# A seven-product gate/up block with a row's sign turned: weight sums as pure additions, two of four made by accumulating DMAs

## The chip, the cores and the metric

The kernel runs on one core of a Trainium2 chip. The metric is device time in microseconds (us) of one execution, the median of several. Five engines work side by side, each with its own queue that runs in order: TensorE (PE, matmuls), VectorE (DVE), ScalarE (ACT), GpSimd (POOL) and SyncE (SP, which here only issues DMAs). Semaphores order work between engines.

## The reference

The reference is one layer of a hybrid trunk: a Mamba-2 part and a latent-attention part side by side, an output projection, and a dense SwiGLU feed-forward part, run for 512 prompt tokens and 64 sample tokens. All data is float32. What matters here is the feed-forward part, with D_MODEL = 1024 and D_FF = 2816:

```python
hf = rmsnorm(x, p['norm_ffn'])
x = x + (jax.nn.silu(hf @ p['w_gate']) * (hf @ p['w_up'])) @ p['w_down']
```

## The kernel before

**Layout.** The 576 tokens lie along the free axis and the model dimension along the 128 partitions. D_FF is cut into 22 tiles of 128, f = 0 to 21. The token axis is cut into two halves of 288.

**Float32 from two parts.** Each matmul operand is split into a high part (a cast to float32r by ACT, line 112) and a low part (what is left, by DVE, line 113). A product is then three matmuls: high by high, high by low, low by high. `split_weights` makes the two parts of a [128, 1024] weight block; their tiles are called `wh_...` and `wl_...`.

**The block form.** For a tile f, gate and up of both token halves are a 2x2 by 2x2 block product: rows are gate and up, the inner blocks are the even and the odd blocks of the model dimension, and the columns are the token halves. The kernel does it with seven block products in place of eight. Call the weight blocks A11, A12 (gate, even and odd) and A21, A22 (up). Four weight sums are needed:

- S1 = A21 + A22 (line 809, left half of tile `s1`)
- S3 = A21 − A11 (line 810, left half of tile `s2`)
- S2 = S1 − A11 (line 811, right half of `s1`)
- S4 = A12 − S2 (line 812, right half of `s2`)

All four are DVE instructions of 128x512. `gu_weights(f)` loads the up row (tile `r2`, line 806) and then the gate row (`r1`, line 807), 512 KB each, both from SP, makes the sums, and splits three groups of two blocks: (A11, A12), called `gu_A`, then (S1, S2) and then (S3, S4), both shown as `gu_S`; A22 is split by itself into `gu_a` (lines 814 and 820). The sums of the activations are made once, in `x_operands` (lines 783 to 801).

**Order of the products.** `gu_steps(f)` gives the steps of a tile: m1 (A11), then m4 (A22) and m3 (S4) of the tile before, which are done late, then m6 (S2), m7 (S3), m2 (A12) and m5 (S1). m1, m6, m5 and m3 add up in one PSUM bank, `ps_x`, with a copy (ACT: L914, L918) or an add (DVE: L931, L939) between them; m7 and m4 share `ps_z`; m2 has `ps_y`. Each product is 12 matmuls of 288 columns, so a tile has 84.

**Parts.** CUTS = (0, 5, 10, 14, 18, 22) groups the tiles in parts. After each part follows its down projection (lines 953 and 966), whose weights `wr_d` SP loads too; its results are added to x2 by DVE (L966). After the last part come the last norm and the outputs.

**Buffers.** Raw rows and sums share a pool of seven [128, 1024] slots, `wpool`; the split parts share eleven slots, `w2pool`. A load waits until the slot that it reuses is free, that is, until the split that read it last is done. For f = 0 the raw tiles come from `w2pool`.

**What sets the order.** Each engine runs its instructions in one fixed order. `ISSUE` lists the first stretch of it by hand for each engine (PE up to about the first three tiles of gate/up, and the like for DVE, ACT, POOL and SP); behind that, the tile scheduler orders the rest at build time from its own estimate of durations. POOL has little to do here: DMAs and memsets early, and part of the last norm. A DMA issued from POOL goes through POOL's software queue.

Of the kernel before, what the change touches and what calls it, by code (L numbers as in the profile page):

```python
# [14 lines left out]
ALU = mybir.AluOpType  # L15
# [4 lines left out]
P = 128  # L20
# [34 lines left out]
def hybrid_layer_kernel(ctx: ExitStack, tc: tile.TileContext, a, o):  # L55
    nc = tc.nc
    pe, act, dve, pool, sp = nc.tensor, nc.scalar, nc.vector, nc.gpsimd, nc.sync
# [6 lines left out]
    def close(p):  # L64
        p.__exit__(None, None, None)
# [3 lines left out]
    wpool = ctx.enter_context(tc.tile_pool(name="wpool", bufs=7))  # L69
# [10 lines left out]
    def tmp(name, w=T):  # L80
        return tpool.tile([P, UPW], F32, tag="t", name=name)[:, :w]

    def halves(ap):
        return ap.rearrange("p (a b) -> p a b", a=2)
# [14 lines left out]
    def col(c):  # L99
        return par[:, c : c + 1]  # L100
# [4 lines left out]
    def wslot(wp, name, dt=F32):  # L105
        return wp.tile([P, 1024], dt, tag="w", name=name)

    def split_weights(raw, name, wp=None):

        n = raw.shape[1]  # L110
        hi, lo = (wslot(wp or wout[0], f"{z}_{name}", F32R)[:, :n] for z in ("wh", "wl"))
        act.copy(hi, raw)  # L112
        dve.tensor_tensor(lo, raw, hi.bitcast(F32), ALU.subtract)  # L113
        return hi, lo
# [122 lines left out]
    for z, n, v, k0 in ((0, T, -1e30, 0), (1, NKEY, 1.0, 64)):  # L237
        m = qk_bufs[0][z][96:100]
        pool.memset(m, v)
        for sign in (1, -1):  # L240
            pool.affine_select(
                out=m, in_=m, pattern=[[0, 2], [sign, n]], compare_op=ALU.is_ge, fill=0.0,
# [53 lines left out]
    for hf in range(2):  # L296
        cols = slice(hf * TH, (hf + 1) * TH)
        for z, r0, n in ((k1, 0, 24), (k2, 32, 16)):
            r = slice(64 * hf + r0, 64 * hf + r0 + n)
# [26 lines left out]
    dt, e, s1, qq, acc = g1("dt"), g1("sp_e"), g1("sp_s"), g1("sp_q"), g1("sp_a")  # L326
# [427 lines left out]
    def load_x2():  # L754
# [8 lines left out]
        ORDER_ATT, g=gate, N=norm_y, y=cat_tile, X=load_x2, S=scores, T=turn, t=turn_s, V=values, W=values_s,  # L763
# [11 lines left out]
    w2pool = ctx.enter_context(tc.tile_pool(name="w2pool", bufs=11, reuse_waits="tile"))  # L775
# [7 lines left out]
    def x_operands(kp):  # L783
        last = len(xops) == 3
        if last:
            close(y_)
            pl = ctx.enter_context(tc.tile_pool(name="xop_last", bufs=1, reuse_waits="tile"))
        z = (pl if last else xop).tile([P, 2, 7, TH], F32, name=f"xop{kp}")
        zr = z.bitcast(F32R)
        e, d, t13, t24 = (tmp(f"xv{kp}_{i}").rearrange("p (a b) -> p a b", a=2) for i in range(4))  # L790
        for i, v in enumerate((e, d)):
            act.activation(v, halves(x2[2 * kp + i]), AF.Identity, scale=col(C_NF + 2 * kp + i))
        dve.tensor_tensor(t13[:, 0], e[:, 1], e[:, 0], ALU.subtract)
        dve.tensor_tensor(t13[:, 1], e[:, 1], d[:, 1], ALU.subtract)
        dve.tensor_tensor(t24[:, 0], d[:, 1], t13[:, 0], ALU.subtract)
        dve.tensor_tensor(t24[:, 1], d[:, 0], t24[:, 0], ALU.subtract)
        for v, r in ((e[:, :1], XB11), (d, XB21), (t13, XT1), (t24, XT2)):
            r = slice(r, r + v.shape[1])
            act.copy(zr[:, 0, r], v)
            dve.tensor_tensor(zr[:, 1, r], v, z[:, 0, r], ALU.subtract)  # L800
        xops[kp] = zr

    def gu_weights(f):

        r1, r2, s1, s2 = (wslot((w2pool, wpool)[f > 0], f"gu{f}_{z}") for z in range(4))
        sp.dma_start(r2, a["w_gu"][f, :, 1])
        gu_dma.append(sp.dma_start(r1, a["w_gu"][f, :, 0]).ins)
        l, r = (lambda z: z[:, :512]), (lambda z: z[:, 512:])
        dve.tensor_tensor(l(s1), l(r2), r(r2), ALU.add)
        dve.tensor_tensor(l(s2), l(r2), l(r1), ALU.subtract)  # L810
        dve.tensor_tensor(r(s1), l(s1), l(r1), ALU.subtract)
        dve.tensor_tensor(r(s2), r(r1), r(s1), ALU.subtract)
        a22 = wslot(w2pool, f"gu{f}_a22", F32R)
        act.copy(l(a22), r(r2))
        out = {"A22": (l(a22), r(a22))}
        for names, w in (("A11", "A12"), r1), (("S1", "S2"), s1), (("S3", "S4"), s2):
            w = split_weights(w, f"gu{f}_{names[0]}", wp=w2pool)
            for i, n in enumerate(names):
                out[n] = tuple(z[:, 512 * i : 512 * i + 512] for z in w)
        dve.tensor_tensor(r(a22), r(r2), l(a22).bitcast(F32), ALU.subtract)  # L820
        return out

    w_gu, squared, gu_dma = {}, [], []
# [22 lines left out]
    def block_product(ps, w, i, kps=KPS, first=True, last=True, onto=False):  # L846

        n, xi = PRODUCTS[i - 1]
        for kp in kps:
            (whi, wlo), x = wk(w[n], kp), xops[kp][:, :, xi]  # L850
            for j, (p, q) in enumerate(((whi, x[:, 0]), (whi, x[:, 1]), (wlo, x[:, 0]))):
                pe.matmul(  # L852
                    ps, p, q, start=not onto and first and kp == kps[0] and j == 0,
                    stop=onto or (last and kp == kps[-1] and j == 2), skip_group_check=onto,
                )

    def fbank(tag, name):
        return bank(tag, name)[:, :TH]
# [5 lines left out]
    def combine(i, ps, g, u):  # L864

        gl, gr, ul, ur = g[:, :TH], g[:, TH:], u[:, :TH], u[:, TH:]
        if i == 1:
            act.copy(gl, ps)
            return
        for out, other in {6: ((ul, gl),), 2: ((gl, gl),), 5: ((ur, ul),), 3: ((gr, ur),), 7: ((ur, ur), (ul, ul)), 4: ((ul, ul),)}[i]:  # L870
            dve.tensor_tensor(out, other, ps, ALU.add)

    ORDER = (1, 6, 2, 5, 3, 7, 4)

# [22 lines left out]
    def finish(f, g, u):  # L897
        act.activation(g, g, AF.Silu)
        dve.tensor_tensor(u, u, g, ALU.mult)
        s = slot(cpool, "c", f"pr{f}")  # L900
        split_scaled(s, u, None)
        prod[f] = hilo(s)

    def gu_steps(f):


        w = w_gu.pop(f) if f in w_gu else gu_weights(f)
        g, u = tmp(f"g{f}"), tmp(f"u{f}")
        gl, gr, ul, ur = g[:, :TH], g[:, TH:], u[:, :TH], u[:, TH:]
        x, y, z = fbank("sc", f"ps_x{f}"), fbank("pp", f"ps_y{f}"), fbank("pp", f"ps_z{f}")  # L910

        def m1():
            block_product(x, w, 1)
            act.copy(gl, x)  # L914

        def m6():
            block_product(x, w, 6, onto=True)
            act.copy(ul, x)  # L918

        def m7():  # L920
            block_product(z, w, 7)
            act.copy(ur, z)

        def m2():
            block_product(y, w, 2)
            dve.tensor_tensor(gl, y, gl, ALU.add)
            dve.tensor_tensor(gl, gl, R2[:, :TH], ALU.mult)

        def m5():
            block_product(x, w, 5, onto=True)  # L930
            dve.tensor_tensor(ur, x, ur, ALU.add)  # L931

        def m4():
            block_product(z, w, 4, onto=True)
            dve.tensor_tensor(ul, z, ul, ALU.add)

        def m3():
            block_product(x, w, 3, onto=True)
            dve.tensor_tensor(gr, x, R2[:, TH:], ALU.mult)  # L939
            finish(f, g, u)  # L940

        return m1, (m4, m3), (m6, m7, m2, m5)

    wout[0] = w2pool
# [87 lines left out]
    ps = [lbank(tag, f"ps_l0_{t}", 0) for t, tag in enumerate(("hm", "hm", "sc", "pp"))]  # L1032
    for t in range(4):
        down_half(ps[t], last_terms(t)[:-1], parts[0], True, False)
    for t in range(KT):
        if t < 4:
            p = ps[t]
            down_half(p, last_terms(t)[-1:], parts[0], False, True)
        else:
            p = lbank(("hm", "sc", "pp")[t % 3], f"ps_l0_{t}", 0)  # L1040
            down_half(p, last_terms(t), parts[0])
        add(t, 0, p)
        z = sql[:, parts[0]] if t == 1 else tmp("sq", parts[0].stop)
# [25 lines left out]
    with tc.manual_schedule(engines={pe.engine, dve.engine, pool.engine, act.engine}):  # L1069
        pn0, pn1 = lbank("sc", "ps_n3_0", 0), bank("pp", "ps_n3_1")[:, : len(BL)]  # L1070
        first, second, _ = norm_steps(pn0, pn0, D, eps=False)
# [10 lines left out]
        for t in range(KT):  # L1082
            p = lbank(("hm", "sc", "pp")[t % 3], f"ps_l1_{t}", 1)
# [20 lines left out]
        first, second, _ = norm_steps(Rt, pn1, D, eps=False)  # L1104
# [32 lines left out]
def issue_in_order(tc, nc):  # L1137
# [45 lines left out]
292-293 296 309 312 304 326 305 310 308 313 327 362 311 328 322 301 323 314 363 330 324 320 329 315 336 321 325 364  # L1183
333 367 337 331-332 365 340 338 334-335 341 344 349 339 345 350 342 346 352 351 343 355 358 366 347 359 357 348 360
356 353 361 368 377 354 370-371 369 372 375-376 373-374 382 390 378 384 383 385-386 379 389 387 380 397 388 381 393
405 395 391 396 398 394 392 400 399 401 403 402 420 406 404 408 407 409 412 410 417 414 411 413 418 462 416 421 423
419 464 425 422 424 415 433 431 426 432 429 428 427 438 430 434 469 463 436 435 437 439 442 441 443 466 440 444 451
465 446 467-468 452-453 445 447 455 454 448 473 475 456 477 476 474 457 472 470 478 458 449 479 488 459 490 485 492
480 489 491 471 450 503 481 505 493-494 482 460 495 487 500 507 504 496 506 518 461 508 502 510 568 575 545 509 512
483 525 511 497 520 519 501 522 486 484 573 521 515 513 517 548 523-524 570 498 530 537-538 527 543 516 526 565 499  # L1190
542 528 555 540 560 514 529 532 553 547 552 557 533 562 541 539 534 550 577 558 531 563 579 578 544 580 535
""",
    "ACT": """
0-5 8 6-7 10 9 13 11 14 12 15 17-18 16 21 19 24 20 23 40 22 25 44 26-27 51 28-33 48-49 55 34-35 37 36 59 50 41-42
# [10 lines left out]
350 359 375 370 367 369 368 376-378 371 379-380  # L1205
""",
    "POOL": """
0-3 7 18 28 4 8 5 9 6 10 26 11 27 12 29 13-17 20-23 19 24-25 31 30 32-42 53 55 57 59 54 56 58 60 43-52 61-73
""",
    "SP": """  # L1210
11-14 16 15 17-20 23 22 25 21 24 31 26 32 39-40 36 33 38 41-42 37 43-47 55 77 62 79 54 56 58 63 81 57 60 59 61 68 66
# [102 lines left out]
```

## Time and profile before

| | |
|---|---|
| median of 3 runs | 654.88 us (653.42 to 655.2) |
| span of the profiled execution, first to last instruction | 651.7 us |
| mean granted TensorE clock | 0.997 |
| PE, DVE, ACT, POOL busy | 639.9, 512.4, 339.3, 41.3 us |
| DMA traffic | 63.22 MB, mean 97 GB/s |

The page gives the profiled execution's time as its span, 651.7 us; some 3.2 us of the median lie outside the first and last instruction. A row of an engine's timeline has the start in us, the duration in us, the engine, the line, the operation, the tiles as out<-in, the shape and the count; in brackets stands how long the engine had been idle before it and which instruction ended that. A row of a group of instructions has count and mean duration; a row of DMA issues has the size of one and the median time from issue to landing.

### The profile page before, as it was taken

The numbers are of one execution on the slowest core, as the hardware profiler recorded it, in microseconds if no ns is written. First come the engines' busy times: TensorE is split into PE (matmuls) and PEld (weight loads), VectorE is DVE, ScalarE is ACT, GpSimd is POOL, SyncE is SP. The second block draws the span as 40 slices with busy tenths as digits, with TensorE's granted clock in tenths as the row PEclk, the third lists the DMA queues.
The fourth block names the chain that finished last, engine by engine and source line by source line (L and its number), as shares of the span: only waits on it lengthen the run. The fifth ranks groups of instructions, "written<-read, shape, count | busy, mean of one in ns | idle before, by whom it ended". The sixth has DMA issues, their size and how long they took to land.

```text
span 651.7 us, 11921 instructions
## 1 busy us (share of the span) xinstructions
PE 639.9 (98%) x4731; PEld 611.8 (94%) x4731; DVE 512.4 (79%) x935; ACT 339.3 (52%) x630; POOL 41.3 (6%) x80
## 2 busy tenths in 40 slices
PE   9999999998999999999999999999999999999995
PEld 8898989885787899999999999999999999999995
DVE  6899987899776699999996776775768577876655
ACT  7645426769674567665523445223533345334364
POOL 1321104001010000000000000000000000000023
PEclk9999999999999999999999999999999999999998
DMA  8312375323220232133422233311232224222004
GB/s 314 127 62 70 93 171 143 113 66 129 86 76 33 99 102 92 65 109 103 131 80 97 79 101 101 110 66 65 81 114 98 98 66 128 68 98 98 2 1 145
DMA packets 26151, 63.22 MB, mean 97 GB/s; under 512 B 3418, under 2 KB 10088, under 8 KB 25840
## 3 DMA queue, kind: packets, MB, share of 16 engines
q1 hardware_dynamic: 24560, 60.77, 28.3%
q0 software_dynamic: 816, 1.13, 0.8%
q8 instruction: 37, 0.61, 0.4%
q10 hardware_dynamic: 720, 0.57, 0.3%
q14 instruction: 18, 0.15, 0.1%
HBM read 58.03 MB, written 3.30 MB: 94 GB/s over the span
## 4 chain that ended last, share of the span: by engine, by line
PE 84%; DVE 3%; ACT 1%; DMA 1%; issue 1%; POOL 0%; POOLq 0%; DVEq 0%; ACTq 0%
PE ps_x L852 21%; PE ps_d L953 18%; PE ps_z L852 10%; PE ps_o L443 8%; PE ps_y L852 5%; PE ps_in L128 4%; PE ps_z L443 3%; PE ps_l L953 3%; PE ps_p L852 2%; PE sc L657 2%; PE pv L704 1%; PE ptp L679 1%; PE ps_v L590 1%; PE ps_q L443 1%; PE ps_y L527 1%
## 5 line engine op out<-in xcount | busy, mean ns | idle before, releaser
L953 PE MATMUL ps_d<-pr,wh_d 128*128 128x288 f32 x576 | 115.4, 294 | 0.0
L852 PE MATMUL ps_x<-xop,wh_gu_S 128*128 128x288 f32 x504 | 101.8, 295 | 0.0
L953 PEld LDWEIGHTS ps_d<-pr,wh_d 128*128 128x128 f32 x576 | 92.5, 188 | 0.0
L953 PE MATMUL ps_d<-pr,wl_d 128*128 128x288 f32 x288 | 84.6, 295 | 0.0
L852 PEld LDWEIGHTS ps_x<-xop,wh_gu_S 128*128 128x128 f32 x504 | 80.6, 188 | 0.2
L113 DVE TENSOR_TENSOR wl_gu_S<-gu,wh_gu_S 128x1024 fp32r<-128x1024 f32 x44 | 53.6, 1224 | 34.4 <-PE ps_y L852 13.8
L852 PE MATMUL ps_x<-xop,wl_gu_S 128*128 128x288 f32 x252 | 73.4, 295 | 0.0
L112 ACT CAST wh_gu_S<-gu 128x1024 fp32r<-128x1024 f32 x44 | 46.3, 1052 | 48.4 <-PE ps_d L953 25.4
L953 PEld LDWEIGHTS ps_d<-pr,wl_d 128*128 128x128 f32 x288 | 54.0, 188 | 0.0
L852 PEld LDWEIGHTS ps_x<-xop,wl_gu_S 128*128 128x128 f32 x252 | 47.0, 188 | 0.0
L128 PE MATMUL ps_in<-xs,wh_in 128*128 128x288 f32 x256 | 45.2, 298 | 1.2 <-DVE sp_a L351 1.0
L112 ACT CAST wh_d<-wr_d 128x640 fp32r<-128x640 f32 (+1 forms) x32 | 21.5, 673 | 39.1 <-PE ps_x L852 14.8
L128 PEld LDWEIGHTS ps_in<-xs,wh_in 128*128 128x128 f32 x256 | 37.5, 188 | 2.3 <-ACT up L381 1.2
L852 PE MATMUL ps_z<-xop,gu_a 128*128 128x288 f32 x252 | 38.0, 296 | 0.0
L852 PE MATMUL ps_z<-xop,wh_gu_S 128*128 128x288 f32 x168 | 36.0, 296 | 0.0
L852 PE MATMUL ps_x<-xop,wh_gu_A 128*128 128x288 f32 x168 | 35.3, 298 | 0.0
L852 PEld LDWEIGHTS ps_z<-xop,gu_a 128*128 128x128 f32 x252 | 35.1, 188 | 0.0
L852 PE MATMUL ps_y<-xop,wh_gu_A 128*128 128x288 f32 x168 | 34.2, 294 | 0.0
L966 DVE TENSOR_TENSOR x<-ps_d,x 128x288 f32<-128x288 f32 x64 | 28.8, 453 | 6.7 <-PE ps_d L953 6.5
L112 ACT CAST wh_gu_A<-gu 128x1024 fp32r<-128x1024 f32 x22 | 23.1, 1049 | 17.5 <-PE ps_d L953 11.5
L113 DVE TENSOR_TENSOR wl_gu_A<-gu,wh_gu_A 128x1024 fp32r<-128x1024 f32 x22 | 26.9, 1223 | 5.2 <-PE ps_x L852 3.9
L1049 POOL TENSOR_TENSOR fz<-fz,sq 128x320 f32<-128x320 f32 x3 | 2.6, 880 | 445.3 <-ACT sq L1044 445.3
(339 smaller groups left out, 1643.7 us busy)
## 6 DMA issues: line engine op xcount, KB each, us to landing
gu<-in_w_gu SPq DMA_DIRECT2D x44, 512.0 KB, 3.7
wr_d<-in_w_down SPq DMA_DIRECT2D x16, 320.0 KB, 2.9
wr_in<-in_w_in SPq DMA_DIRECT2D x8, 512.0 KB, 4.0
wr_out<-in_w_out SPq DMA_DIRECT2D x8, 512.0 KB, 3.2
wr_d<-in_w_down SPq DMA_DIRECT2D x16, 256.0 KB, 2.7
cumb<-cumD SPq DMA_DIRECT2D x5, 512.0 KB, 4.6
x<-in_xT SPq DMA_DIRECT2D x2, 1152.0 KB, 7.5
wr_z<-in_w_in SPq DMA_DIRECT2D x4, 512.0 KB, 4.4
```

Source lines behind the costliest of these rows:

```text
L112: act.copy(hi, raw)
L113: dve.tensor_tensor(lo, raw, hi.bitcast(F32), ALU.subtract)
L128: pe.matmul(ps[:m, hf, :n], w, x[:, hf * n : (hf + 1) * n], start=start and k == 0 and i == 0, stop=stop and k == last and i == 2,)
L443: pe.matmul(ps[:, :n], w, x[:, cols], start=k == 0 and i == 0, stop=k == len(terms) - 1 and i == 2,)
L527: pe.matmul(py[64 * j : 64 * j + 64, p * P : p * P + L], xdt[:L, h * HD : (h + 1) * HD], wts[:L, h, :L], start=True, stop=True,)
L590: pe.matmul(ps[:n], l, r, start=j == 0, stop=j == 2)
L657: pe.matmul(s[:, :nk], qs[:, j, q0 : q0 + P], ks[:, j, :nk], start=True, stop=True)
L679: pe.transpose(pp[:, k : k + P], prs[p, i][:, j, b * P : b * P + P], ident)
L704: pe.matmul(pv[64 * j : 64 * j + 64, b * P :], V[b][:, h * HD : (h + 1) * HD], pts[p, b, j], start=b == 0, stop=True, skip_group_check=b > 0,)
L852: pe.matmul(ps, p, q, start=not onto and first and kp == kps[0] and j == 0, stop=onto or (last and kp == kps[-1] and j == 2), skip_group_c ...
L953: pe.matmul(ps, w, x[:, cols], start=first and k == 0 and i == 0, stop=last and k == len(terms) - 1 and i == 2,)
L966: dve.tensor_tensor(x2[t][:, cols], ps, x2[t][:, cols], ALU.add)
```

## The change

A row's sign in the block form is turned, so that all four weight sums become additions: S3 = A21 + A11, S1 = A21 + A22, S2 = S1 + A11, S4 = A12 + S2. The activations' sums and the places where products are folded take the opposite signs (in `x_operands`, `combine`, m5 and m4).

For f = 1 and up, two of the sums are made by DMA. SP loads the left half of the up row (A21) twice, side by side, into a tile `s31`. Then two DMAs on POOL's queue read the left half of gate (A11) and the right half of up (A22) from DRAM and add them onto the left and the right half of `s31`, which then holds S3 and S1. SP loads the gate row (`r1`) as before, and of the up row only the right half (`r2`). DVE makes S2 and S4 in tile `s24`. The groups are split in the order (A11, A12), (S3, S1), (S2, S4). For f = 0 DVE makes all four sums, with the groups as before.

The lists in `ISSUE` are renumbered for the 42 instructions fewer on DVE; POOL's list has its last part renumbered, and the 42 accumulating DMAs are not in it.

```diff
@@ x_operands
-        dve.tensor_tensor(t13[:, 0], e[:, 1], e[:, 0], ALU.subtract)
+        dve.tensor_tensor(t13[:, 0], e[:, 0], e[:, 1], ALU.subtract)
         dve.tensor_tensor(t13[:, 1], e[:, 1], d[:, 1], ALU.subtract)
-        dve.tensor_tensor(t24[:, 0], d[:, 1], t13[:, 0], ALU.subtract)
-        dve.tensor_tensor(t24[:, 1], d[:, 0], t24[:, 0], ALU.subtract)
+        dve.scalar_tensor_tensor(t24[:, 0], t13[:, 0], -1.0, d[:, 1], ALU.mult, ALU.subtract)
+        dve.tensor_tensor(t24[:, 1], d[:, 0], t24[:, 0], ALU.add)
@@ gu_weights
-        r1, r2, s1, s2 = (wslot((w2pool, wpool)[f > 0], f"gu{f}_{z}") for z in range(4))
-        sp.dma_start(r2, a["w_gu"][f, :, 1])
-        gu_dma.append(sp.dma_start(r1, a["w_gu"][f, :, 0]).ins)
         l, r = (lambda z: z[:, :512]), (lambda z: z[:, 512:])
-        dve.tensor_tensor(l(s1), l(r2), r(r2), ALU.add)
-        dve.tensor_tensor(l(s2), l(r2), l(r1), ALU.subtract)
-        dve.tensor_tensor(r(s1), l(s1), l(r1), ALU.subtract)
-        dve.tensor_tensor(r(s2), r(r1), r(s1), ALU.subtract)
+        if f:
+            r1, r2, s31, s24 = (wslot(wpool, f"gu{f}_{z}") for z in range(4))
+            g, u = a["w_gu"][f, :, 0], a["w_gu"][f, :, 1]
+            sp.dma_start(s31.rearrange("p (a b) -> p a b", a=2), l(u).unsqueeze(1).to_broadcast([P, 2, 512]))
+            gu_dma.append(sp.dma_start(r1, g).ins)
+            pool.dma_start(l(s31), l(g), accum_op=ALU.add)
+            pool.dma_start(r(s31), r(u), accum_op=ALU.add)
+            sp.dma_start(r(r2), r(u))
+            dve.tensor_tensor(l(s24), r(s31), l(r1), ALU.add)
+            dve.tensor_tensor(r(s24), r(r1), l(s24), ALU.add)
+            sums = (("S3", "S1"), s31), (("S2", "S4"), s24)
+        else:
+            r1, r2, s1, s2 = (wslot(w2pool, f"gu{f}_{z}") for z in range(4))
+            sp.dma_start(r2, a["w_gu"][f, :, 1])
+            gu_dma.append(sp.dma_start(r1, a["w_gu"][f, :, 0]).ins)
+            dve.tensor_tensor(l(s1), l(r2), r(r2), ALU.add)
+            dve.tensor_tensor(l(s2), l(r2), l(r1), ALU.add)
+            dve.tensor_tensor(r(s1), l(s1), l(r1), ALU.add)
+            dve.tensor_tensor(r(s2), r(r1), r(s1), ALU.add)
+            sums = (("S1", "S2"), s1), (("S3", "S4"), s2)
         a22 = wslot(w2pool, f"gu{f}_a22", F32R)
         act.copy(l(a22), r(r2))
         out = {"A22": (l(a22), r(a22))}
-        for names, w in (("A11", "A12"), r1), (("S1", "S2"), s1), (("S3", "S4"), s2):
+        for names, w in ((("A11", "A12"), r1), *sums):
@@ combine
-            dve.tensor_tensor(out, other, ps, ALU.add)
+            dve.tensor_tensor(out, ps, other, ALU.subtract if i == 7 else ALU.add)
@@ m5
-            dve.tensor_tensor(ur, x, ur, ALU.add)
+            dve.tensor_tensor(ur, ur, x, ALU.subtract)
@@ m4
-            dve.tensor_tensor(ul, z, ul, ALU.add)
+            dve.tensor_tensor(ul, z, ul, ALU.subtract)
@@ ISSUE["DVE"] is renumbered; the last list of ISSUE["POOL"]
-... 43-52 61-73
+... 43-52 61-68 111-115
```

The line numbers of the new kernel that the prediction uses: L811 and L812 are the two accumulating DMAs, L813 the load of up's right half, L814 and L815 the two sums left on DVE.

More of the change, by code (lines that the diff above doesn't have):

```diff
@@ L1185 @@
 356 353 361 368 377 354 370-371 369 372 375-376 373-374 382 390 378 384 383 385-386 379 389 387 380 397 388 381 393
[L1186 to L1191, printed above, removed]
+405 395 391 396 398 394 392 400 399 401 403 402 420 406 404 408 407 409 412 410 417 414 411 413 418 416 421 423 419
+425 422 424 415 433 431 426 432 429 428 427 438 430 434 467 462 436 435 437 439 442 441 443 464 440 444 451 463 446
+465-466 452-453 445 447 455 454 448 456 473 471-472 457 470 468 474 458 449 475 459 481 486 476 484-485 469 450 477
+487-488 478 460 489 483 494 499 497 490 498 461 500 496 502 558 565 535 501 504 479 515 503 491 510 495 512 482 480
+563 511 507 505 509 538 513-514 560 492 520 527-528 517 533 508 516 555 493 532 518 545 530 550 506 519 522 543 537
+542 547 523 552 531 529 524 540 548 521 553 567 534 568 525
 """,
@@ L1207 @@
     "POOL": """
-0-3 7 18 28 4 8 5 9 6 10 26 11 27 12 29 13-17 20-23 19 24-25 31 30 32-42 53 55 57 59 54 56 58 60 43-52 61-73
+0-3 7 18 28 4 8 5 9 6 10 26 11 27 12 29 13-17 20-23 19 24-25 31 30 32-42 53 55 57 59 54 56 58 60 43-52 61-68 111-115
 """,
```

## The prediction

> **What bounds the kernel now.** I read the page's head and chain first, then the stretches of the feed-forward part, then what PE waits for there, and last the few microseconds around the second gate/up tile.
>
> ```profile
> span 651.7 us, 11921 instructions
> PE 639.9 (98%) x4731; PEld 611.8 (94%) x4731; DVE 512.4 (79%) x935; ACT 339.3 (52%) x630; POOL 41.3 (6%) x80
> ...
> PE 84%; DVE 3%; ACT 1%; DMA 1%; issue 1%; POOL 0%; POOLq 0%; DVEq 0%; ACTq 0%
> ```
>
> The chain that ended last is PE for 84% of the span. The table by stretches says how tight PE is where the change lies (columns: stretch and its length, busy time and count on PE, weight loads, DVE, ACT and POOL, clock, DMA share, GB/s):
>
> ```profile
> core 0: us, PE busy (x) PEld busy (x) DVE busy (x) ACT busy (x) POOL busy (x), PEclk, DMA share, GB/s
> 0.00:262.00 262.00, 256.72 (x1854) 229.99 (x1855) 221.38 (x445) 165.13 (x355) 32.07 (x68) 1.00 0.34 110
> 262.00:282.00 20.00, 20.00 (x147) 19.43 (x146) 19.48 (x34) 12.95 (x23) 0.00 (x0) 1.00 0.24 82
> 282.00:634.00 352.00, 352.00 (x2647) 352.00 (x2646) 261.67 (x432) 153.39 (x233) 3.02 (x4) 1.00 0.26 86
> ```
>
> From 282 to 634 us PE is busy all 352.00 us, at the full clock, and 352.00/2647 is 0.133 us for each matmul of 288 columns. It never waits, so a delay put in anywhere is not made good later, and there is nothing to win. Between 262 and 282 us 20.00/0.133 makes 150 matmuls fit where 147 stand: 3 × 0.133 = 0.4 us is all that PE could gain. DVE is 97% busy in those 20 us and 74% busy behind them. So the change can help only by about 0.4 us, and hurts wherever an operand comes later than its first matmul.
>
> **The change part by part.** *Fewer adds.* Two of the four sums of each tile from f=1 leave DVE.
>
> ```profile
> L810 DVE TENSOR_TENSOR gu<-gu,gu x22: 681/686/694, 228.3 to 581.0; 128x512 f32<-128x512 f32 x22
> ...
> DVE gu L810 <- DMA gu<-in_w_gu: 1.0, 2, 0.7
> ...
> 276.04 0.45 DVE L178 SCALAR_TENSOR_TENSOR R<-nr_u,nr_y 128x288 f32<-128x288 f32 x1
> 276.41 0.45 DVE L931 TENSOR_TENSOR u<-ps_x,u 128x288 f32<-128x288 f32 x1
> ```
>
> 42 × 0.686 = 28.8 us less on DVE, all of it under a PE that is busy throughout: worth nothing, up to the 0.4 us above. *Signs.* In x_operands four subtractions become scalar_tensor_tensor; at 128x288 both kinds take 0.45 us, so 0. Add turned to subtract in combine, m4 and m5: the same form, 0.
>
> *Order of the sums: the certain loss.* For f=1 and up the sums are now grouped [S3|S1] first and [S2|S4] second. The product PE does right after m1 is m6, which needs S2. Before, S2 was in the first group split; now it is in the second. In the fixed part of the order the second group's cast stands on ACT behind the copy of m1's result. At f=2 (the tile of m1 at 276 to 278):
>
> ```profile
> 277.14 1.22 DVE L113 TENSOR_TENSOR wl_gu_S<-gu,wh_gu_S 128x1024 fp32r<-128x1024 f32 x1
> ...
> 279.55 1.23 DVE L113 TENSOR_TENSOR wl_gu_S<-gu,wh_gu_S 128x1024 fp32r<-128x1024 f32 x1 [0.45 <-ACT wh_gu_S L112]
> ...
> 278.17 0.40 ACT L914 COPY g<-ps_x 128x288 f32<-128x288 f32 x1 [3.46 <-PE ps_x L852]
> 278.46 1.05 ACT L112 CAST wh_gu_S<-gu 128x1024 fp32r<-128x1024 f32 x1
> ...
> 278.44 0.71 PE L852 MATMUL ps_x<-xop,wh_gu_S 128*128 128x288 f32 x3
> 278.99 0.30 PE L852 MATMUL ps_x<-xop,wl_gu_S 128*128 128x288 f32 x1
> ```
>
> The group split first is ready at 277.14 + 1.22 = 278.36, and m6's first low-part matmul runs at 278.99. The second group's cast begins when the copy behind m1 lets it, ends at 279.51, and its low part at 279.55 + 1.23 = 280.78. That is when S2 is whole in the new kernel: 280.78 − 278.99 = 1.8 us in which PE has nothing else in its order. Nothing of the change shortens this, since ACT waits for PE's own m1 and the removed adds stand elsewhere. It costs from 0.9 us (if only the high part, 279.51 against the third matmul of the row at 278.44, that is about 278.6, held PE) to 1.8 us; I take 1.8, as the low part is the third matmul of the product. What is late next is z's m7 (S3, now early): no further stall. At the later tiles DVE and ACT are further ahead of PE, so I cost this at nothing there; that cover is the slack used below.
>
> *Loads.* SP now issues three DMAs for each tile: left half of up, doubled (512 KB written), gate (512 KB), right half of up (256 KB). Rows for their kinds:
>
> ```profile
> gu<-in_w_gu SPq DMA_DIRECT2D x44, 512.0 KB, 3.7
> ...
> wr_d<-in_w_down SPq DMA_DIRECT2D x16, 256.0 KB, 2.7
> ...
> out_ckvT<-ckf POOLq DMA_DIRECT2D x1, 288.0 KB, 2.5
> ...
> L311 POOL DMA_DIRECT2D out_ckvT<-ckf x1: 592/592/592, 39.4 to 39.4; - x1
> ...
> DMA to landing us min/median/max: 3.5/3.9/5.5
> ```
>
> (the last line is that of the gate loads, L807, which start beside another load). The first two take the places of L806 and L807, released by the same splits of the tile two back. The 21 added issues cost SP 0.33 us each; each stands ahead of the next tile's load and waits for the second group's split two tiles back, which is done well before that load is due (508.0 against 513.32 in the stretch below): 0, and up to the 0.33 us if it is not. The half it loads feeds only A22, used in m4 a tile later: 0.
>
> *Accumulates.* POOL gets 42 of them, in pairs of 256 KB, each pair waiting for the doubled load to land; L814 on DVE waits for the second. POOL has 3.02 us of work between 282 and 634, so its queue holds nothing up: 42 × 0.6 = 25 us there is free. DVE is in order, so behind L814 wait L815, the splits of A and S and the adds that empty the down projection's banks. No row shows an accumulating DMA. From below its landing is 2.5 us (288 KB from POOL); from above, the pair moves 512 KB and reads its target too, so 512 KB + 512 KB: 5.5 us is the slowest 512 KB load, and twice the step from 256 to 512 KB (3.7 − 2.7 = 1.0 us) on top of it gives 7.5. I take 4.7, the middle of 3.9 and 5.5, since the second of a pair is most like a 512 KB load that starts beside another.
>
> Is that in time? The tightest place is a down projection in which DVE prepares two tiles:
>
> ```profile
> 491.56 0.33 SPq L806 DMA_DIRECT2D gu<-in_w_gu  x1
> ...
> 501.62 0.33 SPq L806 DMA_DIRECT2D gu<-in_w_gu  x1
> ...
> 513.32 0.33 SPq L806 DMA_DIRECT2D gu<-in_w_gu  x1
> ...
> 498.63 0.69 DVE L810 TENSOR_TENSOR gu<-gu,gu 128x512 f32<-128x512 f32 x1
> ...
> 500.37 1.22 DVE L113 TENSOR_TENSOR wl_gu_A<-gu,wh_gu_A 128x1024 fp32r<-128x1024 f32 x1
> ...
> 506.75 1.23 DVE L113 TENSOR_TENSOR wl_gu_S<-gu,wh_gu_S 128x1024 fp32r<-128x1024 f32 x1 [0.55 <-ACT wh_gu_S L112]
> ...
> 510.87 0.68 DVE L810 TENSOR_TENSOR gu<-gu,gu 128x512 f32<-128x512 f32 x1
> ...
> 512.07 1.22 DVE L113 TENSOR_TENSOR wl_gu_A<-gu,wh_gu_A 128x1024 fp32r<-128x1024 f32 x1
> ...
> 518.52 0.29 PE L852 MATMUL ps_x<-xop,wl_gu_A 128*128 128x288 f32 x1
> ```
>
> L814 stands where L810 stood. The load at 491.56 leads to the add (498.63), that to the end of the A split behind it (501.59), that to the next load, and once more round to the A split that ends at 513.29, which PE wants at 518.52: 5.2 us of slack. With an accumulate that lands a us after its issue, one round is 3.7 (load) + 2 × 0.6 (issues on POOL) + a + 3.0 (add to split's end), the second has 2.4 for the last term: together 15.2 + 2a. PE allows 518.52 − 491.56 = 27.0, so it is in time up to a = 5.9. At 4.7 there is 2.4 us to spare: 0.
>
> The sum: 0 (adds) + 0 (signs) + 1.8 (S2 at f=2) + 0 (loads) + 0 (accumulates) = +1.8 us, on the profiled execution's span of 651.7 us. The median of the runs shown is 654.88 us, 3.2 us of it outside the span, which the change leaves alone: 656.7 us. By the ends named above (0.9 for the stall and a gain of 0.4; 1.8 and 0.33 for SP) this case alone lies between 655.4 and 657.0.
>
> **The rivals.** *Late accumulates (slower).* Place: L814, with DVE's queue behind it. Speaking for it: DVE's add already waited twice for a load (1.0 us in all), and traffic per tile rises from 1 MB to 1.75 MB. It decides from a = 5.9 on. If all traffic shares the same engines, the pair's 512 KB, as much again for reading its target, and the 512 KB gate load together make six steps of 256 KB; with 2.7 − 1.0 = 1.7 us that does not grow with size, 1.7 + 6 × 1.0 = 7.7 us. Then each such stretch is late by 15.2 + 15.4 − 27.0 = 3.6 us; four parts after the first (starting at f=5, 10, 14, 18) prepare tiles that way: 14.4 + 1.8 = +16.2, 671.1 us. Against it: the gate load is mostly issued 2 to 3 us after the first, so they overlap only in part. The Trainium skill, "DMA: Bandwidth & Descriptors", section "Issuing engines are not separate DMA queues", states that DMAs of scalar, sync and gpsimd end up on the same 16 engines and interleave; by it POOL's pair gets no path of its own, and this rival's 671.1 us is the outcome. The trace agrees in kind: gate loads, which start beside another load, take up to 5.5 us against a median of 3.9; how much an accumulate adds no run here shows.
>
> *DVE relief (faster).* The 1.4 us that leave DVE for each tile let S2 be whole at f=2 in time after all, and close the 0.4 us of gaps: 654.88 − 0.4 = 654.5. It decides only if the copy of m1's result were not ahead of the cast; the ACT rows show it is.
>
> *No stall, no gain (same).* The stall happens but PE's order gives other work, or the split comes early: 654.9. Against it, PE's order is fixed by hand there.
>
> **How the numbers follow.** On time, with the S2 stall: 0.47. Late accumulates: 0.39. No stall: 0.10. Faster: 0.04, of which half comes out beyond 0.3% only by the scatter of the runs (653.42 to 655.2). What a measurement can tell from no change is 0.3%, 2.0 us; the likeliest case at +1.8 straddles that, so 0.24 of its 0.47 counts as same and 0.23 as slower. Faster 0.02; same 0.24 + 0.10 + 0.02 = 0.36; slower 0.23 + 0.39 = 0.62. The range runs from 654.3 (the relief, with 0.2 for its scatter) to 672 (the late case with a = 7.8: 15.2 + 15.6 − 27.0 = 3.8, four times, plus 1.8 is 17.0); beyond it I leave slower accumulates, 0.1, and the rest below.
>
> **What would show it.** Right: PE waits once near 279 us, for an L113 or L112 of the second group, 1 to 2 us, and nowhere else up to the last part; accumulates land 4 to 5.5 us after issue; DVE busy drops by about 29 us and its waits grow at L814 without PE noticing. Wrong: waits of PE on L113 in the tiles near 518 us, DVE waiting at L814 for DMA by several us at a time, accumulates of 6 us and more; or no wait near 279.

## The result and the profile after

The changed kernel takes 695.2 us (median, 693.5 to 696.52) against 654.5 us for the kernel before, run beside it: a ratio of 1.0623, 95% interval 1.0602 to 1.0645. It is 40.7 us slower; the forecast was 656.7 us, and the range ended at 672.

In the new kernel the lines below line 806 are 13 further down: L865 is the gate/up matmul (L852 before), L966 the down matmul (L953), L979 the add that empties a down bank (L966), L952 and L935 the fold of m3 and the copy behind m7 (L939, L922). The head of the page after and its chain:

```profile
span 694.8 us, 12070 instructions
PE 650.5 (94%) x4731; PEld 620.3 (89%) x4731; DVE 483.9 (70%) x893; ACT 338.6 (49%) x630; POOL 79.2 (11%) x122
...
PE 12%; DMA 5%; DVE 3%; issue 2%; POOL 1%; ACT 0%; POOLq 0%; DVEq 0%; SPq 0%; ACTq 0%
```

DVE lost 28.5 us of work and PE is still longer: its 4731 matmuls are the same. The part of the chain that can be followed has fallen from 84% PE to 12% of the span, and DMA is now 5% of the span. What PE waits for from 255 us to the last part (total, times, longest), where before there was not one row:

```profile
PE ps_x L865 <- DVE wl_gu_A L113: 24.7, 8, 6.0
PE ps_d L966 <- DVE x L979: 3.2, 2, 1.9
PE ps_x L865 <- DVE wl_gu_S L113: 0.7, 1, 0.7
PE ps_x L865 <- ACT wh_gu_S L112: 0.6, 1, 0.6
```

The last two rows are the forecast wait at f=2. The first, eight waits for the low split of A, is the main loss. It is odd at first sight, since A is a plain load and no accumulate touches it. The timeline of one stretch of the changed kernel (rows of SP, POOL, DVE and PE) shows why:

```profile
514.03 0.38 SPq L809 DMA_DIRECT2D gu<-in_w_gu  x1
...
529.22 0.38 SPq L809 DMA_DIRECT2D gu<-in_w_gu  x1
...
544.40 0.38 SPq L809 DMA_DIRECT2D gu<-in_w_gu  x1
...
520.27 0.86 POOL L811 DMA_DIRECT2D gu<-in_w_gu  x1 [14.39 <-DMA gu<-in_w_gu]
520.82 1.21 POOL L812 DMA_DIRECT2D gu<-in_w_gu  x1
...
526.28 0.69 DVE L814 TENSOR_TENSOR gu<-gu,gu 128x512 f32<-128x512 f32 x1 [6.83 <-DMA gu<-in_w_gu]
527.00 0.69 DVE L815 TENSOR_TENSOR gu<-gu,gu 128x512 f32<-128x512 f32 x1
527.61 0.45 DVE L979 TENSOR_TENSOR x<-ps_d,x 128x288 f32<-128x288 f32 x1
527.98 1.22 DVE L113 TENSOR_TENSOR wl_gu_A<-gu,wh_gu_A 128x1024 fp32r<-128x1024 f32 x1
...
541.58 0.69 DVE L814 TENSOR_TENSOR gu<-gu,gu 128x512 f32<-128x512 f32 x1 [7.33 <-DMA gu<-in_w_gu]
...
543.16 1.22 DVE L113 TENSOR_TENSOR wl_gu_A<-gu,wh_gu_A 128x1024 fp32r<-128x1024 f32 x1
...
538.03 0.42 PE L865 MATMUL ps_x<-xop,wh_gu_A 128*128 128x288 f32 x2
544.43 0.61 PE L865 MATMUL ps_x<-xop,wl_gu_A 128*128 128x288 f32 x1 [5.99 <-DVE wl_gu_A L113]
```

The doubled load of 514.03 releases the accumulates at 520.27; the second lands just ahead of L814 at 526.28, where DVE has stood idle for 6.83 us. The split of A of the tile before is queued behind L814 and ends at 529.20. That split frees the slot for the next doubled load, at 529.22. So load, two accumulates, sum and split form a ring, in which each step releases the next: 529.22 − 514.03 = 15.2 us, and 544.40 − 529.22 = 15.2 us again. Before, the same loads followed each other after 10.06 and 11.70 us. PE, which needs 84 × 0.133 = 11.2 us for a tile, runs out at 538 us and waits 6.0 us.

The landing times in this ring (rows of L809, the doubled load; L810, the gate load; L812, the second accumulate; each with its landing line):

```profile
L809 SPq DMA_DIRECT2D gu<-in_w_gu x21: 378/379/381, 241.9 to 611.1; - x21
...
DMA to landing us min/median/max: 4.4/5.3/6.9
...
L810 SPq DMA_DIRECT2D gu<-in_w_gu x21: 327/328/459, 242.3 to 613.0; - x21
...
DMA to landing us min/median/max: 3.9/4.9/6.5
...
L812 POOL DMA_DIRECT2D gu<-in_w_gu x21: 1204/1207/1232, 248.7 to 617.6; - x21
...
DMA to landing us min/median/max: 5.3/6.2/7.8
```

Two more losses stand behind that one. After four of the waits PE runs at about half its clock in the next 4 to 5 us (table of stretches; the clock is the third value from the end; the first two stretches begin with 0.8 us at the full clock, hence 0.60):

```profile
395.60:399.70 4.10, 4.10 (x20) 4.10 (x21) 4.10 (x7) 2.64 (x4) 0.00 (x0) 0.60 0.59 152
477.50:481.70 4.20, 4.16 (x20) 4.16 (x21) 3.82 (x6) 1.49 (x3) 0.00 (x0) 0.60 0.49 125
544.80:549.90 5.10, 5.10 (x23) 5.10 (x23) 1.90 (x3) 0.40 (x1) 0.00 (x0) 0.50 0.72 191
626.60:632.00 5.40, 5.40 (x24) 5.40 (x24) 1.92 (x3) 0.40 (x1) 0.00 (x0) 0.51 0.59 194
```

In these 18.8 us 87 matmuls ran where 18.8/0.133 = 141 would fit: 54 × 0.133 = 7.2 us lost. The waits are 29.2 us. And the end of the program, from PE's last matmul on, is 2.5 us longer (the drain, below). Together 38.9 of the 43.1 us by which the span grew (694.8 − 651.7). Most of what is left is a matter of counting: taken from the start of one matmul to the start of the next, the waits come to 31.1 us and the half clock to 8.2 us, which with the 2.5 us at the end leaves 1.3 us.

### The profile page after: what moved, and what is told of

Its sections match the earlier page's. It is cut to its first block, busy times and chain, and to the rows that moved or that the text cites. A ratio compares the mean times of both kernels' runs of the same rounds, so it can differ in the third digit from the quotient of the medians.

```text
span 694.8 us, 12070 instructions
## 1 busy us (share of the span) xinstructions
PE 650.5 (94%) x4731; PEld 620.3 (89%) x4731; DVE 483.9 (70%) x893; ACT 338.6 (49%) x630; POOL 79.2 (11%) x122
## 5 line engine op out<-in xcount | busy, mean ns | idle before, releaser
L966 PE MATMUL ps_d<-pr,wh_d 128*128 128x288 f32 x576 | 115.4, 295 | 3.2 <-DVE x L979 3.2
L865 PE MATMUL ps_x<-xop,wh_gu_S 128*128 128x288 f32 x504 | 103.6, 297 | 0.6 <-ACT wh_gu_S L112 0.6
L966 PEld LDWEIGHTS ps_d<-pr,wh_d 128*128 128x128 f32 x576 | 92.4, 188 | 3.7 <-DVE x L979 3.7
L966 PE MATMUL ps_d<-pr,wl_d 128*128 128x288 f32 x288 | 84.3, 295 | 0.0
L865 PEld LDWEIGHTS ps_x<-xop,wh_gu_S 128*128 128x128 f32 x504 | 82.0, 191 | 0.9 <-ACT wh_gu_S L112 0.8
L814 DVE TENSOR_TENSOR gu<-gu,gu 128x512 f32<-128x512 f32 x21 | 14.5, 691 | 92.6 <-DMA gu<-in_w_gu 73.8
L865 PE MATMUL ps_x<-xop,wl_gu_S 128*128 128x288 f32 x252 | 74.5, 296 | 0.7 <-DVE wl_gu_S L113 0.7
L811 POOL DMA_DIRECT2D gu<-in_w_gu x21 | 18.2, 865 | 398.9 <-DMA gu<-in_w_gu 162.3
L966 PEld LDWEIGHTS ps_d<-pr,wl_d 128*128 128x128 f32 x288 | 53.9, 188 | 0.0
L865 PE MATMUL ps_x<-xop,wl_gu_A 128*128 128x288 f32 x84 | 27.5, 328 | 24.7 <-DVE wl_gu_A L113 24.7
L865 PEld LDWEIGHTS ps_x<-xop,wl_gu_S 128*128 128x128 f32 x252 | 47.9, 190 | 1.0 <-DVE wl_gu_S L113 1.0
L865 PE MATMUL ps_z<-xop,gu_a 128*128 128x288 f32 x252 | 42.7, 310 | 0.0
L865 PEld LDWEIGHTS ps_x<-xop,wl_gu_A 128*128 128x128 f32 x84 | 17.4, 207 | 26.5 <-DVE wl_gu_A L113 26.5
L865 PEld LDWEIGHTS ps_z<-xop,gu_a 128*128 128x128 f32 x252 | 38.4, 202 | 0.0
L865 PE MATMUL ps_x<-xop,wh_gu_A 128*128 128x288 f32 x168 | 37.5, 312 | 0.0
L865 PE MATMUL ps_z<-xop,wh_gu_S 128*128 128x288 f32 x168 | 36.6, 301 | 0.0
L911 ACT ACTIVATE g<-g 128x576 f32<-128x576 f32 x22 | 15.1, 685 | 43.9 <-DVE g L952 38.9
```

The costliest lines, as they stand in the source:

```text
L811: pool.dma_start(l(s31), l(g), accum_op=ALU.add)
L814: dve.tensor_tensor(l(s24), r(s31), l(r1), ALU.add)
L865: pe.matmul(ps, p, q, start=not onto and first and kp == kps[0] and j == 0, stop=onto or (last and kp == kps[-1] and j == 2), skip_group_c ...
L966: pe.matmul(ps, w, x[:, cols], start=first and k == 0 and i == 0, stop=last and k == len(terms) - 1 and i == 2,)
```

## The experiments

**The signs alone.** The edit, against the kernel before, is the additions and the turned folds, with whole loads and the old groups:

```diff
-        dve.tensor_tensor(l(s2), l(r2), l(r1), ALU.subtract)
-        dve.tensor_tensor(r(s1), l(s1), l(r1), ALU.subtract)
-        dve.tensor_tensor(r(s2), r(r1), r(s1), ALU.subtract)
+        dve.tensor_tensor(l(s2), l(r2), l(r1), ALU.add)
+        dve.tensor_tensor(r(s1), l(s1), l(r1), ALU.add)
+        dve.tensor_tensor(r(s2), r(r1), r(s1), ALU.add)
...
```

> The turned signs alone: whole rows loaded, all four sums on DVE as additions, groups (S1, S2) and (S3, S4) as before. The signs cost nothing: 654.5, PE without a wait from 262 to 634 us. Rival (scalar_tensor_tensor or the subtractions in place of additions are dearer somewhere): 655.5 or more.

654.96 us against 654.28: ratio 1.0007 (0.9991 to 1.0022), and no wait of PE from 262 to 634 us. The signs cost nothing that can be measured.

**Signs and groups, sums on DVE.** The new groups with whole loads and four DVE additions (the list `ISSUE["DVE"]` is renumbered for the two more additions of each tile):

```diff
-            sp.dma_start(s31.rearrange("p (a b) -> p a b", a=2), l(u).unsqueeze(1).to_broadcast([P, 2, 512]))
...
-            pool.dma_start(l(s31), l(g), accum_op=ALU.add)
-            pool.dma_start(r(s31), r(u), accum_op=ALU.add)
-            sp.dma_start(r(r2), r(u))
...
+            sp.dma_start(r2, a["w_gu"][f, :, 1])
...
+            dve.tensor_tensor(r(s31), l(r2), r(r2), ALU.add)
+            dve.tensor_tensor(l(s31), l(r2), l(r1), ALU.add)
...
```

> The signs and the new groups (S3, S1) and (S2, S4) alone, with all four sums on DVE and both rows loaded whole, as before. Main theory (the loss lies in the chain of the accumulating DMAs, and only the one wait at f=2 comes from the order of the groups): 1.6 us over the kernel before, about 656, one wait of PE near 279 us. Rival (the new order of the groups or the scheduler's new order of the rest costs at the later tiles too): 665 or more, with waits of PE on the splits of A beyond 340 us.

658.72 against 654.46 us: ratio 1.0063 (1.0039 to 1.0087). PE's waits from 255 us on:

```profile
PE ps_z L865 <- ACT u L935: 1.4, 1, 1.4
PE ps_x L865 <- ACT wh_gu_S L112: 0.8, 1, 0.8
PE ps_x L865 <- DVE wl_gu_S L113: 0.7, 1, 0.7
```

The wait at f=2 is there, and one that neither theory had: 1.4 us at 297 us, behind ACT's copy of m7's result out of `ps_z`, which stands in ACT's order behind a cast that waited for a sum on DVE. So signs and groups cost 4.3 us in this form, more than the 1.6 forecast; the other 36 of the 40.7 us come only with the accumulating DMAs and the loads that go with them.

**Plain DMAs in place of accumulates.**

```diff
-            pool.dma_start(l(s31), l(g), accum_op=ALU.add)
-            pool.dma_start(r(s31), r(u), accum_op=ALU.add)
+            pool.dma_start(l(s31), l(g))
+            pool.dma_start(r(s31), r(u))
```

> The two accumulating DMAs write in place of adding (S3 and S1 are then plain copies, so this part of the computation is left out); same bytes from DRAM, same queue, same waits, but the target isn't read. If the adding itself is what makes them slow: the second lands in about 4 us after its issue where it took 6.2, a round from load to load shrinks from 15.2 to about 13 us, and the time falls to 660 to 672. If it is the POOL queue and the sharing with the three loads: it lands in about 6 us and the time stays at 690 to 696.

665.3 us, ratio 1.0167 (1.014 to 1.0194). The second DMA of the pair:

```profile
L812 POOL DMA_DIRECT2D gu<-in_w_gu x21: 546/548/558, 250.0 to 591.2; - x21
...
DMA to landing us min/median/max: 3.6/4.3/5.8
```

PE's waits for A in this run:

```profile
PE ps_x L865 <- DVE wl_gu_A L113: 4.5, 3, 2.3
```

The issue of the second DMA on POOL falls from 1.21 to 0.55 us, its landing from 6.2 to 4.3 us, and 29.9 us of the loss go. An accumulating DMA thus lands 1.9 us later than a plain one in this place. The order on DVE is the changed kernel's, and from 408 us on the doubled loads of a part still follow each other after 12.5 to 13.9 us; so a ring longer than PE's 11.2 us remains, but it costs PE three waits in place of eight. The prediction's lower bound, an output of 288 KB that landed in 2.5 us, is no measure even for the plain pair: beside the three loads its second DMA takes 4.3.

**A whole row in place of the doubled load.**

```diff
-            sp.dma_start(s31.rearrange("p (a b) -> p a b", a=2), l(u).unsqueeze(1).to_broadcast([P, 2, 512]))
+            sp.dma_start(s31, u)
...
-            pool.dma_start(r(s31), r(u), accum_op=ALU.add)
+            pool.dma_start(r(s31), l(u), accum_op=ALU.add)
```

> The doubled load of the left half is replaced by one load of the whole up row (the same 512 KB written, 128 runs of 4 KB in place of 256 of 2 KB, and 512 KB read); the second accumulate then adds the left half of up, so the sums are the same. If the doubled load is slow by its form: it lands in about 3.7 us where it took 5.3, a round shrinks by 1.6 us, and at some 16 rounds that PE waits for, up to 25 us go: 670 to 680. If it is slow because of what else is in flight: it lands in about 5.3 us and the time stays at 690 to 696.

687.28 us, ratio 1.0488 (1.0452 to 1.0525); the load of L809:

```profile
L809 SPq DMA_DIRECT2D gu<-in_w_gu x21: 327/328/328, 242.1 to 601.5; - x21
...
DMA to landing us min/median/max: 3.7/3.8/6.4
```

The form of the load was the reason for 5.3 us: the same 512 KB written from whole rows land in 3.8. But the second accumulate became slower (6.6 us in place of 6.2), for a reason that no run here shows, and the gain was 7.9 us, not the 15 to 25 forecast for this case.

**The split of A ahead of L814.** Only DVE's order is changed, from f=7 on. `lows` holds the low splits by name, and the added dependency fixes the order of two instructions of the same engine at build time:

```diff
-            dve.tensor_tensor(l(s24), r(s31), l(r1), ALU.add)
+            s2 = dve.tensor_tensor(l(s24), r(s31), l(r1), ALU.add); f < 7 or tc.add_manual_dep(s2.ins, lows[f"gu{f - 1}_A11"].name, info, reason="issue order")
...
```

> Only the order on DVE: from f=7 on, the low split of A of tile f-1 stands ahead of the sum L814 of tile f, which waits for the accumulates. Main theory (DVE's queue is held at L814 and PE waits for the split behind it, and that split also releases the next tile's load, so that load, accumulate and split make a round of 15.2 us against the 11.2 us that PE needs for a tile): the waits of PE on the split of A go, the loads start earlier, and the time falls to 657 to 665. Rival (the traffic or the accumulates are too slow whatever the order): 685 or more, PE waiting for the splits of S instead.

662.64 us, ratio 1.0134 (1.0103 to 1.0165): 32.6 of the 40.7 us are gone. PE's waits from 255 to 640 us, then the second accumulate:

```profile
PE ps_d L966 <- DVE x L979: 3.2, 2, 1.6
PE ps_x L865 <- DVE wl_gu_S L113: 0.7, 1, 0.7
PE ps_x L865 <- ACT wh_gu_S L112: 0.6, 1, 0.6
```

```profile
L812 POOL DMA_DIRECT2D gu<-in_w_gu x21: 1204/1207/1232, 248.6 to 584.4; - x21
...
DMA to landing us min/median/max: 5.5/7.2/8.5
```

All eight waits for A are gone, with them the half clock, although the accumulates land a whole microsecond later than in the changed kernel. The loads of the part shown above now begin at these times:

```profile
482.35 0.38 SPq L809 DMA_DIRECT2D gu<-in_w_gu  x1
...
497.60 0.38 SPq L809 DMA_DIRECT2D gu<-in_w_gu  x1
...
504.54 0.38 SPq L809 DMA_DIRECT2D gu<-in_w_gu  x1
...
519.48 0.38 SPq L809 DMA_DIRECT2D gu<-in_w_gu  x1
```

From the first to the fourth it is 37.1 us, where the changed kernel's ring takes 45.5 (498.88 to 544.40): the ring is broken once in three rounds. The landing time was not the cause by itself: a split that does not need the accumulates stood behind the one sum that does, and this split released the next load. Nor was the order by itself, since with plain DMAs the same order lost only 10.8 us. It takes the two together. What is left at L814 still holds L979 (3.2 us), the add that empties the down banks.

**S2 first at f=2**, on top of that:

```diff
-            sums = (("S3", "S1"), s31), (("S2", "S4"), s24)
+            sums = ((("S3", "S1"), s31), (("S2", "S4"), s24))[:: -1 if f == 2 else 1]
```

> As the run with the split of A ahead of L814, and at f=2 alone the group (S2, S4) is split ahead of (S3, S1). Main theory (PE's wait near 279 us is for the second group): the wait goes, 1.6 us less than with the split of A ahead alone, about 661. Rival (the sums of (S2, S4) come too late for the first place, or S3 is then late for m7): 662.5 or more, with another wait between 276 and 283 us.

660.92 us, ratio 1.011 (1.008 to 1.014); both rows of the S group are gone from PE's waits. The forecast's step for f=2 is so shown as a wait. The time is 1.7 us less, as forecast, but the intervals of the two runs (1.0103 to 1.0165 before) overlap, so the time alone would not show it.

**One accumulate**, on top of that, with the whole up row loaded as in the run with the row load:

```diff
-            sp.dma_start(s31.rearrange("p (a b) -> p a b", a=2), l(u).unsqueeze(1).to_broadcast([P, 2, 512]))
+            sp.dma_start(s31, u)
...
-            pool.dma_start(l(s31), l(g), accum_op=ALU.add)
-            pool.dma_start(r(s31), r(u), accum_op=ALU.add)
+            pool.dma_start(s31.rearrange("p (a b) -> p a b", a=2), a["w_gu"][f, :, :, :512], accum_op=ALU.add)
```

> As the run with S2 first at f=2, but the whole up row is loaded (512 KB, as in the run with the row load) and one accumulating DMA of 512 KB adds the left halves of gate and up: 21 in place of 42. Theory that POOL's last drain takes 0.083 us for each DMA that POOL has issued (24 before: 2.04 us after its last add; 66: 5.48 us): 45 give 3.7 us, so the end comes 1.8 us earlier; with nothing else changed 659. Rival (the drain goes with the bytes or with the descriptors, which stay the same): 5.5 us of drain, 661.

655.48 us, ratio 1.0012 (0.9998 to 1.0026): no longer to be told from the kernel before, and not faster, as PE has nothing to gain. POOL ends the program with a DRAIN, a row that is longer the more DMAs POOL has issued (min/median/max in ns; the maximum is the one at the end), first in the kernel before, then in the changed kernel, then here:

```profile
L1301 POOLq DRAIN  x3: 46/102/3489, 646.6 to 651.5; - x3
```

```profile
L1314 POOLq DRAIN  x3: 46/98/6922, 687.1 to 694.5; - x3
```

```profile
L1314 POOLq DRAIN  x3: 46/98/5204, 647.7 to 653.4; - x3
```

With 24, 66 and 45 DMAs issued by POOL the drain takes 3.49, 6.92 and 5.20 us: 0.082 us for each on top of some 1.5 us, on a line. The gain of 5.4 us was more than the 2 forecast; 1.7 is the drain, 1.5 that waits behind L979 fell from 2.3 to 0.8 us. The spans of the two profiled executions differ by 4.3 us (658.2 and 653.9), and most of the rest of that is 0.9 us in the last part; the other 1.1 us are scatter, as the profiled execution of the run before lies 1.0 us under its median.

**One accumulate alone**, in the changed kernel with its own order (the two edits to the DMAs above, none to the order).

> The changed kernel with the whole up row loaded and one accumulating DMA of 512 KB, DVE's order and the groups as in the changed kernel. A test of the round: load 3.8 + issue 0.9 or less + accumulate 7.4 (both as in the run that also has the order) + 3.0 on DVE = 14.3 to 15.0 us per tile where the changed kernel has 15.2, so the shorter count of DMAs alone does not help: 675 to 687, PE waiting for the split of A. If the number of DMAs on POOL was what held it: 656 to 660.

682.38 us, ratio 1.0436 (1.0399 to 1.0473). PE waits 17.7 us for the split of A, and the loads into `s31` follow each other every 14.0 to 14.8 us at the end. The ring is what counts: half the POOL DMAs in an unchanged order bring 12.8 us, the order alone 32.6.

**Small DMAs on POOL.** To see the drain by itself, the kernel before with 42 DMAs of 2 KB added:

```diff
+        [pool.dma_start(tiny[:, 4 * i : 4 * i + 4], a["w_gu"][f, :, i, :4]) for i in range(2) if f]
...
```

> The kernel before, with 42 DMAs of 2 KB (16 bytes on each of 128 partitions) added to POOL's queue into a tile that nothing reads, two for each tile from f=1. Theory that each DMA of POOL adds 0.083 us to its last drain: the drain ends 5.5 us after POOL's last add where it ended 2.0 us after it, the end comes 2.5 us later: 657.0. Rival (what counts is the bytes or the adding): 654.5, drain as before.

665.78 us, ratio 1.0161 (1.0116 to 1.0205), outside both forecasts: with no wait on a load, the 42 DMAs ran between 1.4 and 80 us. In POOL's order they stood ahead of the memset of `dt` (L354, at 74.7 us, in the kernel before at 62.1); DVE's `dA` (L356) waited 6.2 us for that memset and PE 5.0 us for `dA`, and PE came 10.5 us later to the feed-forward part. The drain was 6.92 us as expected, but the time says nothing on it. So again, with DMAs that wait for the gate row (the line stands behind the loads):

```diff
-        l, r = (lambda z: z[:, :512]), (lambda z: z[:, 512:])
+        l, r = (lambda z: z[:, :512]), (lambda z: z[:, 512:]); [pool.dma_start(tiny[:, 4 * i : 4 * i + 4], r1[:, 4 * i : 4 * i + 4]) for i in range(2) if f]
...
```

> The kernel before with 42 small DMAs on POOL again, now two for each tile from f=1 that copy a few columns of the gate row once it has landed, so they run between 245 and 580 us and cannot get in the way of the earlier work on POOL. Theory that each DMA of POOL adds 0.083 us to its last drain: 2.5 us more, 656.8, PE without a wait from 262 to 634 us. Rival (the drain hides behind the output DMAs or goes with bytes): 654.3.

656.99 against 654.44 us: ratio 1.0043 (1.0029 to 1.0057), 2.55 us, and PE still has no wait from 262 to 634 us.

```profile
L1301 POOLq DRAIN  x3: 93/179/6924, 646.9 to 654.6; - x3
```

The drain goes with the number of DMAs, not with their bytes: whether the 42 added ones move 2 KB or 256 KB each, it takes 6.92 us.

## Why the prediction was wrong

*Nothing to gain, adds worth nothing, signs worth nothing:* right. DVE fell by 28.5 us (28.8 forecast), and the signs alone and the last repaired kernel cannot be told from the kernel before.

*S2 at f=2, 1.8 us:* right in place, cause and size. PE at that place in the changed kernel:

```profile
278.91 0.29 PE L865 MATMUL ps_x<-xop,wh_gu_S 128*128 128x288 f32 x1
279.75 0.53 PE L865 MATMUL ps_x<-xop,wh_gu_S 128*128 128x288 f32 x2 [0.55 <-ACT wh_gu_S L112]
281.01 0.40 PE L865 MATMUL ps_x<-xop,wl_gu_S 128*128 128x288 f32 x1 [0.73 <-DVE wl_gu_S L113]
```

The third matmul of m6 ran at 281.01 where 278.91 + 3 × 0.133 = 279.31 was due: 1.7 us.

*Loads at 0:* wrong. They are issued when the slots come free, as argued, but the doubled load was priced by the row of a whole-row load of the same size (3.7 us); it lands in 5.3.

*Accumulates at 0, in time up to a = 5.9:* the step that failed. Two things in it were wrong, the sizes and the count. The second landing was taken as 4.7 us and was 6.2, beyond the 5.9 up to which the sum was in time; with the load's 5.3 in place of 3.7 a round became 15.2 us. Two such rounds are 30.4 us against the 27.0 that PE allows, so the sum would have been 3.4 us late in each of four parts, 13.6 us in all. The waits for A and behind L979 are 27.9 us, twice that. What the sizes leave is the count: the sum followed the ring load, accumulate, L814, split, load, and counted it twice round for each part, as if the kernel started level and the slack of 5.2 us were there for two rounds together. Nothing ends the ring after two rounds. From 499 to 544 us it goes round three times at 15.2 us, and what is lost in one round is not made good in the next. It should have been a comparison of periods: 3.7 + 1.2 + 4.7 + 3.0 = 12.6 us by the prediction's own terms, already above PE's 11.2 us for a tile, though by only 1.4 us a round. The run with plain DMAs shows that the count fails even where the sizes are small: with its rows the sum gives 2 × (5.0 + 0.55 + 4.3) + 5.4 = 25.1 us, 1.9 to spare, and PE waited for A all the same.

*The rival of late accumulates* named the place and the sign, and its condition came true (a of 6.2, above 5.9). Its price of 16.2 us was too low by the rounds, by the half clock, and by the drain; and its reason was only part of it. The Trainium skill, "DMA: Bandwidth & Descriptors", section "Issuing engines are not separate DMA queues", has all engines' DMAs interleave on the same 16. The trace agrees: gate loads went from a median of 3.9 to 4.9 us. But an accumulating DMA landed 1.9 us later than a plain one in the same place, where the rival priced it by its bytes alone (7.7 us).

*Not in the forecast at all:* the half clock behind the waits and the drain. The Trainium skill, "TensorE: Matmul & The Clock Gate", section "What's actually happening", states that an idle window of about 3.4 us puts TensorE to half rate. The trace agrees for the waits of about 6 us; it also shows half clock after gaps of 2.6 and 2.8 us from one matmul's start to the next (at 393.0 and 474.7 us), and the full clock after gaps of 3.2 us (at 377.2) and 2.8 us (at 459.5):

```profile
380.40:385.00 4.60, 4.56 (x34) 4.56 (x35) 4.21 (x7) 1.89 (x4) 0.00 (x0) 1.00 0.64 143
462.30:467.00 4.70, 4.67 (x35) 4.67 (x36) 2.49 (x5) 0.53 (x2) 0.00 (x0) 1.00 0.66 143
```

What sorts them is where they fall. In the clock records of each trace the clock changes only at multiples of 3.41 us from one another (in the changed kernel at 396.38, 399.80, 478.30 and 481.71 us, for instance), which divides the time into stretches of that length. The gaps of 2.6 and 2.8 us have 2.60 and 2.65 us in one stretch; the other two are divided into 2.10 + 1.12 and 1.70 + 1.10 us. Between 255 and 640 us of the changed kernel, of the runs with plain DMAs and with the row load, and of the one with one accumulate alone, the half clock follows every gap that has 2.2 us or more in one stretch and no gap that has 2.1 or less in each. So the length of a wait does not give its price, since its place among these stretches decides too.

## What to carry to other kernels

When a sum moves from an in-order engine to a DMA, look at what is queued behind the instruction that now waits for that DMA, and whether something in that queue releases the next DMA: then the latencies add up to a period, to be set against the period of the engine that bounds the kernel, round after round; a slack is there once, not for every round. Moving the one instruction that does not need the DMA ahead of the wait was worth 32.6 us here, about as much as plain DMAs in place of the accumulates (29.9; the two are not clear of each other's scatter), and it keeps the sums right. Where PE never waits, as here, taking 28.5 us of work off another engine bought nothing, and the DMAs put in its place could only cost.

## What the runs showed of the hardware

- POOL's last drain takes 0.082 us for each DMA that POOL issued (3.49, 5.20 and 6.92 us for 24, 45 and 66), the same for 42 added DMAs of 2 KB as for 42 of 256 KB. Here the 42 small ones made the kernel 2.55 us longer.
- The rows of POOL show 0.86 us for the issue of the first accumulating DMA of a pair of 256 KB and 1.21 us for the second, which starts 0.55 us after the first (520.27 and 520.82 us); a plain one takes 0.55. As the second of a pair beside other loads an accumulating DMA lands in 6.2 us, a plain one in 4.3.
- A load that writes each half row twice (runs of 2 KB) lands in 5.3 us; the same bytes from whole rows in 3.8.
- PE's clock changed only at multiples of 3.41 us from one another. Gaps between matmuls were followed by half clock, for 3.4 or 6.8 us, when 2.2 us or more of them fell between two such points (2.60 and 2.65 us at 393.0 and 474.7 us), and not when at most 2.1 did (2.10 of 3.2 us at 377.2).
